# Moving two buffers to the upper end of SBUF and re-planning the Strassen steps of the output projection, in a one-core decoder block

## The chip, the core and the metric

The kernel runs on one core of one Trainium2 chip. The metric is device microseconds of one execution of the whole block. In what follows PE is the matmul engine, DVE the vector engine, ACT the scalar engine, POOL the GpSimd engine (here it mostly issues DMAs), and SP the queue that issues the weight loads. SBUF is the on-chip memory (128 partitions; sizes below are per partition), PSUM the matmul accumulators.

## The reference

One decoder block on 256 tokens of width 4096, all float32:

```python
h = rmsnorm(x, norm_w)
proj = h @ w_in                                  # 4096 -> 20480
u_p, z_p, u_c, b_c, c_c, z_c, g_logit = split(proj)
y_pool = causal_multiscale_pool(u_p, pool_w, pool_scale) * silu(z_p)
y_conv = b_c * causal_conv3(c_c * u_c, conv_w, conv_b) * silu(z_c)
br = [y_pool @ w_branch[0], y_conv @ w_branch[1]]   # 2048 -> 4096 each
merged = sum(sigmoid(g_logit + gate_b) * br)
out = rmsnorm(x + merged @ w_out, final_norm_w)
```

Nearly all of the arithmetic is in the three projections: `w_in`, `w_branch` and `w_out`.

## The kernel before

**Units and steps.** Each projection is cut into units of 1024 output columns; a unit is a run of steps, and a step is one pair of 128-row slices of the contraction against 256 tokens and 1024 columns. There are 20 units of 16 steps for `w_in` (`cz`, `cb`, `cu`, `cc`, `pz`, `pu`, `g`), eight units of 8 steps for `w_branch` (`b0_c`, `b1_c`) and four of 16 steps for `w_out` (`o0` to `o3`). Every float32 operand is split into a rounded high part and a low rest, and a product is three matmuls (high by high, high by low, low by high). A step is of one of two kinds. A "P" step is plain: 8 blocks of 128x128 against 512 columns, so 24 matmuls. An "S" step is a Strassen step (Winograd's form): 7 products, so 21 matmuls, at the price of four sums of weight quarters that DVE makes. The strings at the head of the file (`NINE`, `TEN`, `OUT3`, ...) give the kinds in order; `TEN` has ten S steps of 16, `NINE`, `NINE_A` and `NINE_B` nine, `EIGHT` eight, the old `OUT3` seven.

**Standing operands.** The activations stand in the array (they are the weights in the sense of the engine: LDWEIGHTS loads them, 128x128 at a time), and the weight matrices stream past out of `ring`. The activation operands lie in `arena`, 16 of them at a time: eight with room for a P step (4 KB each), six with 7 KB and two with 8 KB. The very last one has its own tile `last_pair` (8 KB), which is on the right side of SBUF, so it lies at the top end. An S step on one of the P-sized operands finds its four Strassen sums in the tile `side` (4 KB), which holds them for one operand at a time. Of the six with 7 KB, the first unit finds one block each in `extra` (6 KB), a tile that is closed after step 12.

**Places.** The pool `const` holds, in this order, `arena` 82 KB, `ring` 60, `raw` 24, `E` 8, `Y` 8, `sa` 4, `ident` 0.5 and `par` 0.4, together 187 KB. Pools opened later lie behind it: first `extra`, then `parts` (8 KB, the Strassen sums of the weights) and behind that `side`. So counted from the start of the tiles, `arena` and `ring` are the first 142 KB, and `extra`, `parts` and `side` begin at 187 KB or above.

**Weights.** SP loads 1 MB of weights per step into one of three `raw` buffers. ACT rounds it into cells of `ring` (15 cells), DVE writes the low rest beside it. For an S step DVE also makes the sums (`parts<-raw`, `parts<-parts,raw`), ACT rounds them and DVE writes their low rests. The order on ACT and DVE is fixed by the program (`pump` lays down the work up to four steps ahead of the matmul steps, as far as cells and `raw` buffers are free). A `tick` is six matmuls: every six matmuls one item of `queue` is laid down; `queue` holds a unit's epilogue, a list of items and empty places (`gap(n)`), which so runs while the next unit is multiplied.

**Joining a unit with S steps.** The four corner products (`shared` banks) are copied out by ACT into a slot, `corner_sums` combines them there with three DVE instructions, and `combine` adds the slot to the base. There are two ways. With `rotates`, the slot is the next `raw` buffer in its turn, and DVE adds it (`add(d4, d4, q)`). With `late` and not `rotates`, the slot is `Y` or `last_pair`, and two accumulating DMAs on POOL's queue (`gather`, seen as `E<-Y`) do the addition. Before the change all four out units rotate and are added by DVE.

**Side sums.** `side_items(i)` loads the columns of operand `i` (`sa<-in_xc`, POOL's queue), scales them (ACT), forms the four sums (`sums_s`, four DVE instructions) and writes high and low parts to `side` (ACT, DVE). It is run for operand 7 in the epilogue of `cz0`, for use in the `NINE` units; `pz0` then closes `side` for other tiles. In the epilogue of `g0_0`, while `g1_0` is multiplied, it runs for operand 6 and then for operand 7, each followed by a store to `side_d` in DRAM; the `TEN` units then reload one of the two between their first and last S step.

**The out units.** `o0` has SIX5 (six S steps), `o1` and `o2` EIGHT, `o3` OUT3. The epilogue gathers the rows of `x` onto `E` (`row`), takes the sums of squares (`square`, ACT), multiplies by the final norm's weights in `Y[:, 0]` and stores to `o_d`. `start` loads these weights into `Y[:, 0]`, three quarters into the unit. The last three P steps of `o3` are the tail, run first for tokens 0 to 127 and then for the others, each followed by `finish`.

Of the kernel before, what the change touches and what calls it, by code (L numbers as in the profile page):

```python
# [9 lines left out]
F32 = mybir.dt.float32  # L10
# [32 lines left out]
NINE_B = "PSPSPSPSSPSSPSPS"  # L43
HOST = "PPPBPPMMPSPSSPSSPSS"
TEN = "PSPSSPSSPSSPSSPS"
OUT3 = "PSPSPSPSPSPSSPPP"
B0 = "PPPPSPSP"
B1 = "PSPSPSPP"
B1_LAST = "PSPPSPPP"
# [3 lines left out]
def hybrid_block(ctx: ExitStack, tc: tile.TileContext, x, xc, prm, rows_in, w_in, pool_w, w_branch, w_out, out):  # L53
# [17 lines left out]
    def sub(dst, a, b):  # L71
        return tt(dst, a, b, ALU.subtract)
# [10 lines left out]
    def move(dst, src):  # L83
        return pin(nc.gpsimd.dma_start(dst, src))
# [2 lines left out]
        return pin(nc.gpsimd.dma_start(dst, src, accum_op=ALU.add))  # L87

    const = ctx.enter_context(tc.tile_pool(name="const", bufs=1))
    PSUM = bass.MemoryType.PSUM  # L90
    psum = ctx.enter_context(tc.tile_pool(name="psum", bufs=1, space=PSUM))
    dram = ctx.enter_context(tc.tile_pool(name="dram", bufs=1, space=bass.MemoryType.DRAM))

    def sb(name, shape, dt=F32):
        return const.tile(shape, dt, name=name)

    arena = sb("arena", [P, (4 * ND + 7 * NS + 8 * (NB - 1)) * KB], F32R)
    ring = sb("ring", [P, CELLS, 2, NH], F32R)
    raw = sb("raw", [P, NRAW, 2 * NU])
    E = sb("E", [P, 2, NU])  # L100
    Y = sb("Y", [P, 2, NU])
    sa = sb("sa", [P, 8, P])
    ident = sb("ident", [P, P])
    par = sb("par", [P, 112])
# [131 lines left out]
    def quarters(tile_):  # L236
        return tile_.rearrange("p a (b c) -> p (a b) c", c=NH)
# [239 lines left out]
    def gap(n):  # L477
        return [None] * n
# [38 lines left out]
    def in_unit(name, col, epi, text, **kw):  # L517
        units.append(Unit(name, lambda i: w_in[col // NU, i], seq_x(text), x_ops, epi, scaled=True, **kw))
        units[-1].text = text
        return units[-1]  # L520

    def side_items(i=ND - 1):
        def scaled():
            for k in range(2):
                v = sa[:, 6 - 2 * k:8 - 2 * k]
                act(v, v, scale=norm_col(2 * i + k))

        return [lambda: move(sa[:, 4:].rearrange("p o c -> p (o c)"), xc[i])] + gap(7) + [scaled, None, lambda: sums_s(sa)] + gap(3) + [
            lambda: act(side["tile"][:, 0], sa[:, 0:4]), None,
            lambda: sub(side["tile"][:, 1], sa[:, 0:4], side["tile"][:, 0].bitcast(F32))]  # L530

    def silu_y(late):
        def silu(t):
            act(Y[:, t], Y[:, t], AF.Silu, **(dict(scale=rin[:, t:t + 1]) if late else {}))
        return gap(18 if late else 3) + [lambda: silu(0), None, lambda: silu(1)]
# [5 lines left out]
    def conv_units(c, first):  # L541
        base = 2 * HALF + c * NU

        def b_epi(u):
            def copy(j):
                act(chan(Y)[:, 2 * j:2 * j + 2], bankview(j))
            return gap(6) + transposes(E, copy) + [lambda: move(g_d[c], Y)]

        def c_epi(u):
            def copy(j):  # L550
                if j == 3:
                    for i in range(4):
                        act(chan(E)[:, 2 * i:2 * i + 2], bankview(i))

            def taps(j):
                v, y = chan(E)[:, 2 * j:2 * j + 2], chan(Y)
                for i in range(2):
                    b = 2 * j + i
                    kb = 8 * c + b
                    act(y[:, b], v[:, i], AF.Identity, scale=tap_col(2, kb), bias=bias_col(kb))  # L560
                for s in (1, 2):
                    for i in range(2):
                        b = 2 * j + i
                        kb = 8 * c + b
                        stt(y[:, b, s:], v[:, i, 0:T - s], tap_col(2 - s, kb), y[:, b, s:], ALU.mult, ALU.add)

            items = gap(6) + pairs(transposes(E, copy)) + gap(1)
            for j, n in enumerate((1, 7, 8, 8)):
                items += gap(n) + [lambda j=j: taps(j)]
            return items + [lambda: move(E, g_d[c])] + gap(6) + [lambda: mul(E, E, Y), lambda: put(y_d[1, c], chan(E))]  # L570

        u = in_unit(f"cz{c}", base + 3 * HALF, lambda u: silu_y(u.late) + (gap(4) + side_items() if first else []),
                    FIRST if first else SIX4, dst=Y)
        u.rotates, u.late = first, not first
        in_unit(f"cb{c}", base + HALF, b_epi, NINE_B if c else NINE_A).urgent = lambda: mul(E, E, Y)
        u = in_unit(f"cu{c}", base, lambda u: rescale(Y), EIGHT3, dst=Y)
        u.late, u.rotates = True, False
        in_unit(f"cc{c}", base + 2 * HALF, c_epi, NINE_A).urgent = lambda: mul(E, E, Y)
# [101 lines left out]
    def gate_unit(n, c):  # L680
        def epi(u):
            def bias(t):
                gather(E[:, t], gate_b[n, None, c * NU:(c + 1) * NU].to_broadcast([P, NU]))

            pause = gap(12)
            if (n, c) == (1, 3):
                pause = gap(5) + [lambda: move(Y, gates_d[0, 0])] + gap(6)
            items = (rescale(E) if u.late else gap(1)) + [lambda: bias(0), lambda: bias(1)] + pause + [
                lambda: act(E[:, 0], E[:, 0], AF.Sigmoid), None,
                lambda: act(E[:, 1], E[:, 1], AF.Sigmoid), lambda: move(gates_d[n, c], E)]  # L690
            if (n, c) == (0, 0):
                sides = []
                for i in range(ND - 2, ND):
                    sides += side_items(i) + [lambda i=i: move(side_d[i - ND + 2], side["tile"])]
                items += gap(len(sides) - len(items))
                items = [lambda a=a, b=b: (a and a(), b and b()) for a, b in zip(items, sides + gap(len(items)))]
            return items
        text = HOST if (n, c) == (0, 0) else SEVEN3 if (n, c) == (1, 3) else NINE if (n, c) == (1, 0) else TEN
        u = in_unit(f"g{n}_{c}", 6 * HALF + n * D + c * NU, epi, text)
        u.rotates, u.late = False, (n, c) != (1, 3)  # L700

    def spare():
        return last_pair["tile"].rearrange("p (a n) -> p a n", a=2)
# [30 lines left out]
    def out_unit(c):  # L734
        cs = slice(c * NU, (c + 1) * NU)

        def start():
            move(Y[:, 0], final_w[None, cs].to_broadcast([P, NU]))

        def epi(u):  # L740
            def row(t):
                gather(E[:, t], xrows[:, t, cs])

            def square(t):
                act(Y[:, 1], E[:, t], AF.Square, accum_out=ossq[:, t, c:c + 1])
            return gap(1) + [lambda: row(0), lambda: row(1)] + gap(14) + [
                lambda: square(0), lambda: square(1),
                lambda: mul(E, E, Y[:, 0:1].to_broadcast([P, 2, NU])), lambda: move(o_d[c], E)]

        text = (SIX5, EIGHT, EIGHT, OUT3)[c]  # L750
        units.append(Unit(f"o{c}", lambda i: w_out[c, i], seq_x(text), m_ops, epi, before=start))

    def sums_s(st):
        sub(st[:, Q5], st[:, A21], st[:, A22])
        sub(st[:, Q6], st[:, Q5], st[:, A11])
        sub(st[:, Q7], st[:, A11], st[:, A21])
        add(st[:, Q3], st[:, A12], st[:, Q6])
# [335 lines left out]
    for u in units:  # L1093
        if u.name == "b0_0":
            last_pair["stack"].close()
            open_last(F32)
        if not u.rotates:
            u.join.slot = quarters(Y if u.name[0] == "g" else spare() if u.name[0] == "b" else E)
        if u is names["g1_0"]:
            bands_open.close()  # L1100
            open_side()
        if u is last_x:
            side["stack"].close()
            more = ctx.enter_context(tc.tile_pool(name="more", bufs=1))
            stages.append(more.tile([P, 8, P], F32, name="sb"))
            queue_fills()
        if u is last:
            break
        for st in u.steps:
            assert st.prepared, (u.name, st.kind)  # L1110
            run_step(u, st)
            if u.text is TEN and st.kind == "S" and st.op in x_ops[:ND] and st is not u.steps[-1]:
                move(side["tile"], side_d[ND - 1 - x_ops.index(st.op)])
            state["now"] += 1
            if state["now"] == OPENED:
                opening.close()
                sums = ctx.enter_context(tc.tile_pool(name="parts", bufs=1)).tile([P, 4, NH], F32, name="parts")
                open_side()
            pump()
            if u.before and st is u.steps[len(u.steps) * 3 // 4]:  # L1120
                flush()
                u.before()
        flush()
        combine(u)
        queue.extend(u.epi(u))
        pump()
# [102 lines left out]
```

## Time and profile before

| | us |
|---|---|
| median of 3 runs | 2378.26 (2377.94 to 2379.73) |
| the profiled execution, own time | 2378.31 |
| its span in the profile | 2376.6 |
| PE busy | 2358.6 |
| DVE busy | 2178.6 |
| ACT busy | 1519.3 |
| POOL busy | 116.8 |

The span runs from the first to the last instruction; the own time of the execution is 1.7 us longer. The four busy times are of engines that run beside each other. A busy PE in the profile means that a matmul is in its pipeline, not that matmuls follow each other as closely as they can.

### The profile page before, as it was taken

What the parts mean: (1) busy time and instruction counts of PE and PEld (TensorE: products, weight loads), DVE (VectorE), ACT (ScalarE), POOL (GpSimd) and SP (SyncE); (2) the same over time, 40 slices, a digit from 0 to 9 for tenths busy, and PEclk for the clock granted to TensorE, in tenths of its full rate; (3) what the DMA queues carried; (4) which work ended last, traced back from release to release, by engine and by line L of the source; (5) the groups of instructions that cost most, each with busy time, mean ns of one, the idle gap of its engine ahead of it and who ended that gap; (6) DMA issues with size and microseconds to landing.
All of it is one profiled execution on the core that took longest, in us unless ns stands there. A gap on an engine that the chain in (4) does not pass through costs nothing.

```text
span 2376.6 us, 28235 instructions
## 1 busy us (share of the span) xinstructions
PE 2358.6 (99%) x10466; PEld 1945.8 (82%) x10466; DVE 2178.6 (92%) x2378; ACT 1519.3 (64%) x1801; POOL 116.8 (5%) x181
## 2 busy tenths in 40 slices
PE   9999999999999999999999999999999999999998
PEld 7888888888888888888788888888888888888886
DVE  8889989989989969969899999998898799899998
ACT  6666656756656656656676767667665566566664
POOL 0000000000001000000000000001100000000000
PEclk9999999999999999999999999999999999999999
DMA  9656646756657546746877787778766666767767
GB/s 344 230 193 235 223 164 260 238 191 236 224 178 269 211 174 221 240 174 217 259 248 251 264 260 250 248 272 274 267 253 242 248 237 239 257 211 252 259 218 267
DMA packets 91322, 564.20 MB, mean 237 GB/s; under 512 B 10096, under 2 KB 10352, under 8 KB 30256
## 3 DMA queue, kind: packets, MB, share of 16 engines
q1 hardware_dynamic: 69824, 485.39, 56.5%
q0 software_dynamic: 20784, 75.77, 11.9%
q8 instruction: 82, 1.34, 0.2%
q10 hardware_dynamic: 576, 1.24, 0.1%
q14 instruction: 56, 0.46, 0.1%
HBM read 522.51 MB, written 27.26 MB: 231 GB/s over the span
## 4 chain that ended last, share of the span: by engine, by line
PE 94%; DVE 3%; DMA 1%; ACT 1%; issue 0%; POOL 0%; SPq 0%; DVEq 0%; ACTq 0%; POOLq 0%
PE sums L1021 69%; PE shared L1021 23%; DVE ring L63 1%; PE shared L665 1%; PE shared L458 1%; DMA sa<-in_xc_dram 1%; DVE parts L63 1%; DMA raw<-in_w_in_dram 1%; ACT ring L60 0%; DVE E L63 0%; DVE raw L63 0%; ACT E L60 0%; DVE E L75 0%; ACT raw L60 0%; PE shared L641 0%
## 5 line engine op out<-in xcount | busy, mean ns | idle before, releaser
L1021 PE MATMUL sums<-ring,arena 128*128 128x512 f32 x7215 | 1687.1, 390 | 4.2 <-DVE ring L63 1.8
L1021 PEld LDWEIGHTS sums<-ring,arena 128*128 128x128 f32 x7215 | 1352.8, 188 | 288.4 <-DVE ring L63 3.1
L63 DVE TENSOR_TENSOR ring<-raw,ring 128x1024 fp32r<-128x1024 f32 (+3 forms) x879 | 971.9, 1126 | 137.2 <-ACT ring L60 136.1
L60 ACT ACTIVATE ring<-raw 128x1024 fp32r<-128x1024 f32 (+3 forms) x682 | 796.2, 1202 | 251.7 <-PE sums L1021 101.2
L60 ACT ACTIVATE ring<-parts 128x512 fp32r<-128x512 f32 (+1 forms) x638 | 476.5, 761 | 475.1 <-DVE parts L63 413.8
L1021 PE MATMUL shared<-ring,arena 128*128 128x512 f32 x2169 | 523.2, 389 | 0.3 <-DVE ring L63 0.3
L63 DVE TENSOR_TENSOR ring<-parts,ring 128x1024 fp32r<-128x1024 f32 (+1 forms) x442 | 492.0, 1158 | 6.1 <-ACT ring L60 6.1
L1021 PEld LDWEIGHTS shared<-ring,arena 128*128 128x128 f32 x2169 | 407.0, 188 | 85.5 <-DVE ring L63 0.8
L63 DVE TENSOR_TENSOR parts<-parts,raw 128x512 f32<-128x512 f32 x416 | 286.6, 689 | 0.0
L63 DVE TENSOR_TENSOR parts<-raw 128x1024 f32<-128x1024 f32 x208 | 254.0, 1221 | 5.5 <-DMA raw<-in_w_in_dram 5.4
L1021 PE MATMUL sums<-ring,last_pair 128*128 128x512 f32 x336 | 84.6, 396 | 0.8 <-DVE ring L63 0.8
L1021 PEld LDWEIGHTS sums<-ring,last_pair 128*128 128x128 f32 x336 | 63.1, 188 | 16.3 <-DVE ring L63 1.2
L1021 PE MATMUL shared<-ring,last_pair 128*128 128x512 f32 x192 | 47.6, 397 | 0.0
L1021 PEld LDWEIGHTS shared<-ring,last_pair 128*128 128x128 f32 x192 | 36.1, 188 | 8.7
L60 ACT ACTIVATE E<-sums 128x512 f32<-128x512 f32 x72 | 39.7, 595 | 5.5 <-PE sums L1021 3.6
L60 ACT ACTIVATE E<-sums,rin 128x512 f32<-128x512 f32 x28 | 17.7, 689 | 29.3 <-PE sums L1021 29.3
L1021 PE MATMUL shared<-ring,side 128*128 128x512 f32 x135 | 34.0, 396 | 0.0
L63 DVE TENSOR_TENSOR raw<-raw 128x512 f32<-128x512 f32 (+1 forms) x27 | 23.5, 870 | 9.8 <-ACT raw L60 8.9
L1021 PEld LDWEIGHTS shared<-ring,side 128*128 128x128 f32 x135 | 25.4, 188 | 6.0
L60 ACT ACTIVATE last_pair<-shared 128x512 f32<-128x512 f32 x44 | 23.9, 596 | 9.4 <-PE shared L458 8.9
L63 DVE TENSOR_TENSOR E<-E,Y 128x2048 f32<-128x2048 f32 x13 | 29.8, 2290 | 0.1
L63 DVE TENSOR_TENSOR E<-E,last_pair 128x2048 f32<-128x2048 f32 x12 | 27.4, 2286 | 2.2 <-ACT E L60 2.2
(134 smaller groups left out, 717.1 us busy)
## 6 DMA issues: line engine op xcount, KB each, us to landing
raw<-in_w_in_dram SPq DMA_DIRECT2D x318, 1024.0 KB, 4.9
raw<-in_w_branch_dram SPq DMA_DIRECT2D x64, 1024.0 KB, 4.9
raw<-in_w_out_dram SPq DMA_DIRECT2D x64, 1024.0 KB, 5.1
E<-in_rows_dram POOLq DMA_DIRECT2D x16, 512.0 KB, 9.8
gates_d<-E POOLq DMA_DIRECT2D x8, 1024.0 KB, 6.1
E<-Y POOLq DMA_DIRECT2D x14, 512.0 KB, 8.2
Y<-E POOLq DMA_DIRECT2D x10, 512.0 KB, 8.1
y_d<-E POOLq DMA_DIRECT2D x8, 512.0 KB, 6.4
```

The lines of the kernel that those rows point to most:

```text
L60: return pin(nc.scalar.activation(dst, src, func, **kw))
L63: return pin(nc.vector.tensor_tensor(out=dst, in0=a, in1=b, op=op))
L458: pin(nc.tensor.transpose(shared(j)[:, i * T + t * P:i * T + (t + 1) * P], src[:, t, c:c + P], ident))
L665: pin(nc.tensor.matmul(o, a, b, start=(k, i) == (0, 0), stop=(k, i) == (3, 2)))
L1021: pin(nc.tensor.matmul(ps, lhs, rhs, start=n == 0, stop=n == u.total[b] - 1))
```

## The change

It has four parts.

1. `raw` and `Y` (32 KB) leave `const` for a pool on the right side of SBUF, at its upper end. `const` is 155 KB then, so `extra`, `parts` and `side` lie 32 KB lower, and `last_pair`, which is also on the right, lies 32 KB lower too, under the two.
2. `side_items` now always ends with a store to `side_d`. The sums of operand 7 are stored in the epilogue of `cz0`. In the epilogue of `g0_0` only operand 6 is computed, after a gap of 14 ticks, stored, and operand 7 is reloaded.
3. `o0`, `o1`, `o2` no longer rotate: their slot is `Y`, and they are joined by accumulating DMAs. `start` moves into their epilogue (tick 16), and the squares from tick 17 to tick 25.
4. `o1` and `o2` get `NINE` in place of `EIGHT`, and `o3` eight S steps in place of seven, three of them in a row before the tail. For the ninth, `o1` computes the side sums of the merged activations' operand 7 while it is multiplied; `more` (a stage for operands) is closed to make room.

```diff
-OUT3 = "PSPSPSPSPSPSSPPP"
+OUT3 = "PSPSPSPSSPSSSPPP"
...
+    upper = ctx.enter_context(tc.tile_pool(name="upper", bufs=1, side="right"))
...
-    raw = sb("raw", [P, NRAW, 2 * NU])
+    raw = upper.tile([P, NRAW, 2 * NU], F32, name="raw")
     E = sb("E", [P, 2, NU])
-    Y = sb("Y", [P, 2, NU])
+    Y = upper.tile([P, 2, NU], F32, name="Y")
...
+    def side_load(i):
+        move(side["tile"], side_d[i - ND + 2])
+
-    def side_items(i=ND - 1):
+    def side_items(i):
...
-            lambda: sub(side["tile"][:, 1], sa[:, 0:4], side["tile"][:, 0].bitcast(F32))]
+            lambda: sub(side["tile"][:, 1], sa[:, 0:4], side["tile"][:, 0].bitcast(F32)),
+            lambda: move(side_d[i - ND + 2], side["tile"])]
...
             if (n, c) == (0, 0):
-                sides = []
-                for i in range(ND - 2, ND):
-                    sides += side_items(i) + [lambda i=i: move(side_d[i - ND + 2], side["tile"])]
-                items += gap(len(sides) - len(items))
+                sides = gap(HUSH) + side_items(ND - 2) + [lambda: side_load(ND - 1)]
...
-            return gap(1) + [lambda: row(0), lambda: row(1)] + gap(14) + [
+            return gap(2) + [lambda: row(0), lambda: row(1)] + gap(12) + [start] + gap(8) + [
                 lambda: square(0), lambda: square(1),
                 lambda: mul(E, E, Y[:, 0:1].to_broadcast([P, 2, NU])), lambda: move(o_d[c], E)]
 
-        text = (SIX5, EIGHT, EIGHT, OUT3)[c]
-        units.append(Unit(f"o{c}", lambda i: w_out[c, i], seq_x(text), m_ops, epi, before=start))
+        text = (SIX5, NINE, NINE, OUT3)[c]
+        u = Unit(f"o{c}", lambda i: w_out[c, i], seq_x(text), m_ops, epi, before=start if c == 3 else None)
+        u.late, u.rotates = c < 3, c == 3
+        units.append(u)
...
-            u.join.slot = quarters(Y if u.name[0] == "g" else spare() if u.name[0] == "b" else E)
+            u.join.slot = quarters(Y if u.name[0] in "go" else spare() if u.name[0] == "b" else E)
+        if u is names["o1"]:
+            assert not fills
+            more.close()
+            open_side()
+
+            j, items = ND - 1, list(queue)
+            queue.clear()
+            sides = (gap(HUSH) + [lambda: move(sa[:, 4:].rearrange("p o c -> p (o c)"),
+                                                   m_d[j // 4][:, j % 4].rearrange("p k t -> p (k t)"))] + gap(8) + [
+                lambda: sums_s(sa), None, None, lambda: act(side["tile"][:, 0], sa[:, 0:4]), None,
+                lambda: sub(side["tile"][:, 1], sa[:, 0:4], side["tile"][:, 0].bitcast(F32))])
+            items += gap(len(sides) - len(items))
+            sides += gap(len(items) - len(sides))
+            queue.extend([lambda a=a, b=b: (a and a(), b and b()) for a, b in zip(items, sides)])
```

More of the change, by code (lines that the diff above doesn't have):

```diff
@@ L570, in c_epi @@
             return items + [lambda: move(E, g_d[c])] + gap(6) + [lambda: mul(E, E, Y), lambda: put(y_d[1, c], chan(E))]
-        u = in_unit(f"cz{c}", base + 3 * HALF, lambda u: silu_y(u.late) + (gap(4) + side_items() if first else []),
+        u = in_unit(f"cz{c}", base + 3 * HALF, lambda u: silu_y(u.late) + (gap(4) + side_items(ND - 1) if first else []),
                     FIRST if first else SIX4, dst=Y)
@@ L1103, in hybrid_block @@
             side["stack"].close()
-            more = ctx.enter_context(tc.tile_pool(name="more", bufs=1))
-            stages.append(more.tile([P, 8, P], F32, name="sb"))
+            more = ExitStack()
+            ctx.enter_context(more)
+            stages.append(more.enter_context(tc.tile_pool(name="more", bufs=1)).tile([P, 8, P], F32, name="sb"))
             queue_fills()
@@ L1112, in hybrid_block @@
             if u.text is TEN and st.kind == "S" and st.op in x_ops[:ND] and st is not u.steps[-1]:
-                move(side["tile"], side_d[ND - 1 - x_ops.index(st.op)])
+                side_load(2 * ND - 3 - x_ops.index(st.op))
             state["now"] += 1
```

## The prediction

> **What bounds the kernel now.** I read the page's busy times and its chain first, then the matmul groups with shapes kept apart, then PE's timeline inside one undisturbed unit, then the stretches unit by unit, and last the waits where a unit took longer than its count of matmuls.
>
> ```profile
> PE 2358.6 (99%) x10466; PEld 1945.8 (82%) x10466; DVE 2178.6 (92%) x2378; ACT 1519.3 (64%) x1801; POOL 116.8 (5%) x181
> PE 94%; DVE 3%; DMA 1%; ACT 1%; issue 0%; POOL 0%; SPq 0%; DVEq 0%; ACTq 0%; POOLq 0%
> ```
>
> PE is never idle for long and holds 94% of the chain, so only three things can move the time: fewer matmuls, matmuls that follow each other more closely, and the few places where PE waits. DVE at 92% is the engine that can turn into the bound.
>
> The groups of matmuls, by the tile that stands in the array (columns: count, then busy time and mean duration):
>
> ```profile
> L1021 PE MATMUL sums<-ring,arena 128*128 128x512 f32 x7215 | 1687.1, 390 | 4.2 <-DVE ring L63 1.8 <-ACT E L60 1.4 <-DVE ring L760 1.1
> L1021 PE MATMUL shared<-ring,arena 128*128 128x512 f32 x2169 | 523.2, 389 | 0.3 <-DVE ring L63 0.3
> L1021 PE MATMUL sums<-ring,last_pair 128*128 128x512 f32 x336 | 84.6, 396 | 0.8 <-DVE ring L63 0.8
> L1021 PE MATMUL shared<-ring,last_pair 128*128 128x512 f32 x192 | 47.6, 397 | 0.0
> L1021 PE MATMUL shared<-ring,side 128*128 128x512 f32 x135 | 34.0, 396 | 0.0
> L1021 PE MATMUL sums<-ring,side 128*128 128x512 f32 x45 | 13.0, 396 | 0.0
> L1021 PE MATMUL sums<-ring,extra 128*128 128x512 f32 x36 | 10.4, 396 | 0.0
> ```
>
> All are 128x128 against 512 columns from `ring`. With `arena` standing one takes 389 to 390 ns, with `last_pair`, `side` or `extra` 396 to 397. These three tiles have nothing in common but their place: behind 187 KB of tiles or at the top end, where `arena` and `ring` lie in the first 142 KB. Durations overlap in the pipeline, so the cost is read from the starts (columns: start, time, then count). Near the end of unit `g1_2`:
>
> ```profile
> 1429.07 2.88 PE L1021 MATMUL shared<-ring,arena 128*128 128x512 f32 x12
> 1431.79 0.84 PE L1021 MATMUL sums<-ring,arena 128*128 128x512 f32 x3
> 1432.47 1.56 PE L1021 MATMUL sums<-ring,last_pair 128*128 128x512 f32 x6
> 1433.88 2.98 PE L1021 MATMUL shared<-ring,last_pair 128*128 128x512 f32 x12
> 1436.69 0.86 PE L1021 MATMUL sums<-ring,last_pair 128*128 128x512 f32 x3
> 1437.39 6.32 PE L1021 MATMUL sums<-ring,arena 128*128 128x512 f32 x27
> 1443.55 0.86 PE L1021 MATMUL sums<-ring,side 128*128 128x512 f32 x3
> ```
>
> Twelve on `arena` take 1431.79 - 1429.07 = 2.72 us, 226.7 ns each; twelve on `last_pair` 1436.69 - 1433.88 = 2.81 us, 234.2 ns. So 7.5 ns more each. The 27 behind them on `arena` take 6.16 us where 27 x 226.7 ns is 6.12, so a little (0.04 us) spills over onto what follows.
>
> The stretches of single units (columns: length, then PE, PEld, DVE, ACT, POOL busy):
>
> ```profile
> 1121.11:1205.78 84.67, 82.38 (x358) 66.71 (x357) 76.32 (x89) 56.64 (x70) 7.04 (x9) 1.00 0.75 243
> 1205.78:1286.43 80.65, 80.65 (x356) 66.46 (x354) 80.58 (x90) 56.85 (x71) 5.31 (x6) 1.00 0.78 255
> ...
> 2119.26:2201.01 81.75, 81.75 (x361) 67.58 (x360) 77.00 (x82) 51.96 (x64) 2.88 (x4) 1.00 0.70 240
> ...
> 2282.81:2365.10 82.29, 82.29 (x364) 67.94 (x362) 77.37 (x85) 47.80 (x61) 3.58 (x5) 1.00 0.73 258
> ```
>
> These are `g1_0`, `g0_1`, `o1` and `o3`. In `g0_1` DVE is busy 80.58 of 80.65 us and PE still never idles: a full DVE is not yet a stall. `g1_0` has three matmuls more than `g0_1` (357 against 354 weight loads), worth 0.68 us, but takes 4.02 us more: 3.3 us are lost there. Why, the chain and the waits of that unit say:
>
> ```profile
> 1128.08 14.92 DMA sa<-in_xc_dram
> ...
> 1143.08 0.91 ACT L60 ACTIVATE sa<-sa,par 128x256 f32<-128x256 f32 x2 [8.08 <-DMA sa<-in_xc_dram]
> ...
> 1145.40 0.69 DVE L63 TENSOR_TENSOR ring<-raw,ring 128x512 fp32r<-128x512 f32 x1 [7.35 <-ACT ring L60]
> ...
> PE sums L1021 <- DVE ring L63: 1.9, 3, 0.8
> ```
>
> The load of `sa` for the side sums is queued on POOL behind the two joining transfers of `g0_0` and lands 14.9 us after its issue. ACT, which works in order, waits 8.08 us for it with the scaling, DVE then waits 7.35 us for ACT's rounding of weights, and PE runs dry in the steps after.
>
> **Part 1: places.** The slow tiles serve 336 + 192 + 135 + 45 + 36 = 744 matmuls; at 7.5 ns that is 5.6 us, and with a part of what spills over behind 24 runs on `last_pair` (24 x 0.04 = 1.0 at most) I take 6.0. All of it is on the path, since PE is the path. The change moves each of the three tiles down by the 32 KB of `raw` and `Y`. Counted from the start of the tiles `extra` comes to 155 KB and `side` to 163. Before, `const`, `parts`, `side` and `last_pair` stood at once, 187 + 8 + 4 + 8 = 207 KB, so the top is at 207 or little above, and `last_pair` comes to about 168 to 176. The rows show fast places up to 142 KB and slow ones from 187 to the top; the tiles land between, so the bounds are 0 and -6.6 us. There are two levels and no slope (389 or 390 anywhere in 142 KB, 396 or 397 in all three high tiles), which looks like a border and not like distance. Every slow tile is shifted by 32 KB, one and a half times the 20 KB that are seen slow; they all clear the border if the slow stretch at the top is no longer than 32 KB. That it is so short is my choice and not a reading; where it is longer, `last_pair` with 528 of the 744 matmuls is the first to stay in it, and that is the second rival below. The two side steps that `o1` and `o2` gain add no slow matmuls then.
>
> The Trainium skill, "SBUF — State Buffer", section "SBUF size: 192, 224, or 256?", gives 192 KiB of memory per partition for trn1, 224 for trn2, and 16 KiB of that reserved. If the added 32 KiB were the slow part, the border would be at 176 KB of the tiles by these figures (an estimate from that page), `last_pair` would end right under it, and the whole 6.0 would come. The page says nothing of speed, and no tile of the trace that PE multiplies with in its steps lies between 142 and 187 KB.
>
> What goes up is `raw` and `Y`, which PE does not read in its steps. DVE and ACT do; `parts`, which now lies high, is the nearest row for what that costs:
>
> ```profile
> L63 DVE TENSOR_TENSOR ring<-raw,ring 128x1024 fp32r<-128x1024 f32 x515 | 617.2, 1222 | 13.0 <-ACT ring L60 12.7
> L63 DVE TENSOR_TENSOR ring<-parts,ring 128x1024 fp32r<-128x1024 f32 x390 | 460.7, 1221 | 6.1 <-ACT ring L60 6.1
> ```
>
> The same shape takes 1222 ns from the low `raw` and 1221 ns from the high `parts`: I cost the move of the buffers at nothing on DVE.
>
> **Part 2: side sums.** In `g1_0` the second set of sums goes (four small subtractions and one of 128x512 on DVE, 1.7 us there by the rows of part 4), and the scaling comes at tick 22 instead of tick 8. A tick is six matmuls, 1.36 us, so it falls 30 us after the unit's start at 1121.11, in place of 11, while the load still leaves POOL's queue right behind the joining transfers, near 1128, and lands near 1143. ACT's 8.08 us, DVE's 7.35 and so PE's 3.3 us go; DVE had only 76.32 us of work in that unit, so nothing else is late next. Bounds: 0 and -3.4; I take -3.3. Added on POOL: one store in `cb0`, and the reload of `side`, which waits for the store before it and holds up `gates_d<-E` behind it, with some 30 us left to the next writer of `E`; `side` itself is needed only in the last step of `g1_0`. I cost these at nothing.
>
> **Part 3: joins by transfer.** The three DVE additions go (2.28 us each), and the `raw` buffer that the join took is free for weights. PE does not wait at these three boundaries now, so this only makes room on DVE. `E` is complete later, but the squares are later too, by 8 ticks or 11 us.
>
> **Part 4: three more S steps.** Each takes 21 matmuls in place of 24: 9 x 226.7 ns = -2.04 us. DVE pays. What a P and an S step cost it, from consecutive starts in `o2`, and the small pieces:
>
> ```profile
> 2236.26 2.36 DVE L63 TENSOR_TENSOR ring<-raw,ring 128x1024 fp32r<-128x1024 f32 x2
> 2238.53 1.22 DVE L63 TENSOR_TENSOR parts<-raw 128x1024 f32<-128x1024 f32 x1
> ...
> 2244.88 2.35 DVE L63 TENSOR_TENSOR ring<-raw,ring 128x1024 fp32r<-128x1024 f32 x2
> ...
> L63 DVE TENSOR_TENSOR sa<-sa 128x128 f32<-128x128 f32 x60 | 14.7, 287 | 0.8 <-ACT sa L60 0.2
> L63 DVE TENSOR_TENSOR side<-sa,side 128x512 fp32r<-128x512 f32 x3 | 2.1, 687 | 0.0
> L63 DVE TENSOR_TENSOR E<-E,raw 128x2048 f32<-128x2048 f32 x3 | 6.9, 2284 | 0.0
> ```
>
> P: 2238.53 - 2236.26 = 2.27 us. S: 2244.88 - 2238.53 = 6.35 us, against 21 x 226.7 ns = 4.76 us on PE. A P turned into an S costs DVE 4.08 us more. `o1`: 77.00 + 4.08 - 2.28 (join) + 1.7 (side sums: 4 x 0.287, overlapped to 1.0, and 0.69) = 80.5 us, of 357 x 226.7 ns = 80.9 us on PE: full, as in `g0_1`, but not over. `o2` has 1.7 less. `o3`: 77.37 + 4.08 - 2.28 = 79.2 of 81.6, but three S steps in a row stand before the tail. There, before:
>
> ```profile
> 2340.23 2.37 DVE L63 TENSOR_TENSOR ring<-parts,ring 128x1024 fp32r<-128x1024 f32 x2
> ...
> 2345.40 2.88 PE L1021 MATMUL shared<-ring,arena 128*128 128x512 f32 x12
> ...
> 2357.25 0.69 DVE L63 TENSOR_TENSOR E<-sums,E 128x512 f32<-128x512 f32 x1 [1.54 <-PE sums L1021]
> ...
> 2365.51 0.69 DVE L63 TENSOR_TENSOR E<-sums,E 128x512 f32<-128x512 f32 x1 [0.64 <-PE sums L1021]
> ```
>
> DVE finishes the last S step's sums at 2342.60; PE needs the first of them from the fourth product, 0.68 us into the twelve at 2345.40: 3.5 us of room. After the change DVE comes there 4.08 - 2.28 = 1.8 us later and PE 0.68 us earlier: 1.0 us of room stays, no stall. In the tail DVE was 1.54 us early at the first half; it is then 1.8 late against PE's 0.68 early, so the first half is finished 0.26 us later than before, and the last one, which had 0.64 us to wait for PE, gains about 0.4 instead of 0.68: +0.3. For `o1`, whose side sums again stand on DVE before a transfer that is queued behind four accumulating ones, I add 0.4 of a possible 0 to 3.4 (the loss in `g1_0`): its sums come 31 us after the unit's start, the transfer should land there by 25 to 37.
>
> **Sum**, against the profiled execution's own 2378.31 us (its span plus 1.7; the median of the runs shown is 2378.26, the same): -6.0 - 3.3 - 2.04 + 0.3 + 0.4 = -10.6, so 2367.7 us. The unknown ends give 2366 to 2370 for this case.
>
> **Rivals.**
>
> *A wait of the old kind comes back* (in `o1` before the side sums, or in `o3` at the three S steps, or the loss in `g1_0` stays). For it: the transfer in `o1` is behind more traffic than the one in `g1_0`, and DVE has 0.4 us to spare in that unit. Against: 14 ticks of gap, and room on DVE from the join. Price about the same loss as in `g1_0`: 2367.7 + 3.3 = 2371.0.
>
> *The tiles do not land in the fast part*, so the change does not do what it says. For it: no row between 142 and 187 KB. Against: the shift is longer than the stretch seen slow. 2367.7 + 6.0 = 2373.7. The Trainium skill, "TensorE: Matmul & The Clock Gate", section "Step-by-step: what each phase is for", gives the standing operand its own SBUF read port and lets its load run under the matmul before; by that rule the place would not matter at all and this would be the time. The trace disagrees: 234.2 against 226.7 ns.
>
> *Slower: DVE reads `raw` more slowly in its new place.* DVE is full in the five `TEN` units; what it reads from `raw` in them is
>
> ```profile
> L63 DVE TENSOR_TENSOR ring<-raw,ring 128x1024 fp32r<-128x1024 f32 (+2 forms) x169 | 169.1, 1021 | 2.5 <-ACT ring L60 2.5
> L63 DVE TENSOR_TENSOR parts<-parts,raw 128x512 f32<-128x512 f32 x100 | 68.9, 689 | 0.0
> L63 DVE TENSOR_TENSOR parts<-raw 128x1024 f32<-128x1024 f32 x49 | 59.9, 1222 | 0.0
> ```
>
> 298 us (1205.78 to 1609). Each per cent more would go straight onto the path there, 3.0 us, so the gain is used up from 3.6% on; at 5% the time is 2367.7 + 14.9 = 2382.6. Against it stands the pair 1222 and 1221 ns above.
>
> **How the numbers follow.** Forecast 0.63, a new or remaining wait 0.17, tiles still slow 0.13, slower 0.05, a larger gain 0.02. A measurement of this kernel can tell about 0.2%, 4.8 us, from no change, so faster means under 2373.5: the forecast, the first rival, the larger gain and a small part of the second, 0.85; within 0.2% is the rest of the second with an edge of the third, 0.10; slower 0.05. The range runs from the low end of the forecast to the second rival, 2366.0 to 2373.7.
>
> **What would show it.** Right: one mean duration, 389 to 390 ns, for all matmuls of 512 columns whatever stands; `g1_0` at about 81 us with no ACT wait on `sa<-in_xc`; `o1` and `o2` near 81 us with DVE full; 204 matmuls on `side` (24 more), 10457 in all. Wrong: 396 ns on `last_pair` or `side`; DVE means above 1222 ns from `raw`; PE waits on `ring` in `o1` or in the last S steps of `o3`.

## The result and the profile after

| | before | after |
|---|---|---|
| median, us | 2378.57 (2377.71 to 2381.04, 22 runs) | 2374.04 (2372.96 to 2377.54, 22 runs) |
| ratio, 95% interval | | 0.9983 (0.9977 to 0.9989) |
| profiled execution, own time | 2378.31 | 2374.06 |
| span | 2376.6 | 2372.2 |

The change is faster by 4.5 us between the medians; the ratio puts it at 0.17%. The forecast was 2367.7 us, 10.6 us less than before, so 6 us of it did not come. The busy times and the groups of matmuls by standing tile, after:

```profile
PE 2355.7 (99%) x10457; PEld 1944.9 (82%) x10457; DVE 2185.2 (92%) x2389; ACT 1525.0 (64%) x1804; POOL 124.4 (5%) x188
...
L1025 PE MATMUL sums<-ring,arena 128*128 128x512 f32 x7179 | 1679.1, 390 | 3.0 <-ACT E L60 1.4 <-DVE ring L764 1.0 <-DVE ring L63 0.6
L1025 PE MATMUL shared<-ring,arena 128*128 128x512 f32 x2175 | 524.6, 389 | 0.0
L1025 PE MATMUL sums<-ring,last_pair 128*128 128x512 f32 x321 | 81.0, 396 | 0.0
L1025 PE MATMUL shared<-ring,last_pair 128*128 128x512 f32 x204 | 50.6, 397 | 0.0
L1025 PE MATMUL shared<-ring,side 128*128 128x512 f32 x153 | 38.5, 396 | 0.0
L1025 PE MATMUL sums<-ring,side 128*128 128x512 f32 x51 | 14.7, 396 | 0.0
```

There are nine matmuls fewer, as counted. But the tiles that moved 32 KB down are as slow as before: 396 to 397 ns on `last_pair` and `side`. The largest term of the prediction's sum did not come at all. The stretch of `o2` before (the others before are in the prediction), and then those of `g1_0`, `o1`, `o2` and `o3` after (length, then PE, PEld, DVE, ACT, POOL busy):

```profile
2201.01:2282.81 81.80, 81.80 (x362) 67.58 (x361) 76.62 (x80) 51.79 (x63) 2.87 (x4) 1.00 0.69 238
```

```profile
1121.00:1202.21 81.21, 81.21 (x359) 67.05 (x357) 78.56 (x89) 58.15 (x70) 6.38 (x8) 1.00 0.81 264
...
2115.83:2197.04 81.21, 81.21 (x358) 67.04 (x357) 80.07 (x90) 53.84 (x66) 5.86 (x7) 1.00 0.77 258
2197.04:2278.26 81.22, 81.22 (x358) 67.03 (x357) 78.62 (x85) 53.43 (x66) 5.31 (x6) 1.00 0.75 253
2278.26:2359.83 81.57, 81.57 (x361) 67.35 (x359) 77.96 (x87) 48.45 (x60) 6.56 (x8) 1.00 0.77 260
```

`g1_0` gained 84.67 - 81.21 = 3.46 us, `o1` 0.54, `o2` 0.58, `o3` 0.72, and PE is busy through all four. That is 5.3 us; the span gained 4.4, so 0.9 us were given back at the end, in the tail. There DVE adds the joined corner sums (`E<-E,parts`) and then finishes the halves of the last tiles. After:

```profile
2351.21 2.29 DVE L63 TENSOR_TENSOR E<-E,parts 128x2048 f32<-128x2048 f32 x1
...
2353.60 0.69 DVE L63 TENSOR_TENSOR E<-sums,E 128x512 f32<-128x512 f32 x1
...
2361.14 0.68 DVE L63 TENSOR_TENSOR E<-sums,E 128x512 f32<-128x512 f32 x1
...
2343.71 16.51 PE L1025 MATMUL sums<-ring,arena 128*128 128x512 f32 x72
```

The last matmuls before:

```profile
2363.91 1.57 PE L1021 MATMUL sums<-ring,last_pair 128*128 128x512 f32 x6
```

Before, both of these additions (`E<-sums,E`) waited for PE (1.54 and 0.64 us); now neither waits: DVE is the late one. The last matmul ends at 2360.22 us and the span 12.0 us later; before, it ended at 2365.48 us, 11.1 us before the end of the span.

### The profile page after: what moved, and what is told of

Same layout as the page of the kernel before. It is cut to its first block, busy times and chain, and to the rows that moved or that the text cites. A ratio compares the mean times of both kernels' runs of the same rounds, so it can differ in the third digit from the quotient of the medians.

```text
span 2372.2 us, 28256 instructions
## 1 busy us (share of the span) xinstructions
PE 2355.7 (99%) x10457; PEld 1944.9 (82%) x10457; DVE 2185.2 (92%) x2389; ACT 1525.0 (64%) x1804; POOL 124.4 (5%) x188
## 4 chain that ended last, share of the span: by engine, by line
PE 95%; DVE 3%; ACT 1%; DMA 1%; issue 0%; SPq 0%; DVEq 0%; ACTq 0%
PE sums L1025 69%; PE shared L1025 23%; DVE ring L63 1%; PE shared L670 1%; PE shared L459 1%; DVE parts L63 1%; DVE E L63 1%; DMA raw<-in_w_in_dram 1%; ACT ring L60 0%; DVE raw L63 0%; DVE E L75 0%; DMA raw<-in_w_out_dram 0%; ACT E L60 0%; ACT raw L60 0%; PE shared L646 0%
## 5 line engine op out<-in xcount | busy, mean ns | idle before, releaser
L60 ACT ACTIVATE ring<-parts 128x512 fp32r<-128x512 f32 (+1 forms) x647 | 483.4, 761 | 471.6 <-DVE parts L63 410.4
L63 DVE TENSOR_TENSOR ring<-parts,ring 128x1024 fp32r<-128x1024 f32 (+1 forms) x449 | 500.1, 1161 | 6.2 <-ACT ring L60 6.1
L63 DVE TENSOR_TENSOR parts<-parts,raw 128x512 f32<-128x512 f32 x422 | 292.6, 693 | 0.0
L63 DVE TENSOR_TENSOR parts<-raw 128x1024 f32<-128x1024 f32 x211 | 258.6, 1225 | 9.2 <-DMA raw<-in_w_in_dram 5.2
L87 POOL DMA_DIRECT2D E<-Y x20 | 24.3, 1454 | 366.5 <-DVE Y L63 322.6
L60 ACT ACTIVATE Y<-shared 128x512 f32<-128x512 f32 x56 | 30.4, 602 | 4.1 <-PE shared L459 3.4
L63 DVE TENSOR_TENSOR Y<-Y 128x512 f32<-128x512 f32 (+1 forms) x33 | 28.7, 869 | 1.7 <-ACT Y L60 0.2
```

The lines of the kernel that those rows point to most:

```text
L60: return pin(nc.scalar.activation(dst, src, func, **kw))
L63: return pin(nc.vector.tensor_tensor(out=dst, in0=a, in1=b, op=op))
```

## The experiments

**First question: what makes a standing tile slow?** The prediction had read it as place. But the compiled kernels' addresses show a second thing that the slow tiles have in common. `arena` (16512) and `ring` (100480) both start on a multiple of 128 bytes, 128 past a multiple of 256. `extra` and `side` start 192, and `last_pair` 224 bytes past a multiple of 256, before the change and after it, because 32 KB is a multiple of 256. Three kernels with a few bytes of padding tried that, and one tried the side sums alone.

*Kernel before, starts on multiples of 128:*

```diff
     ossq = sb("ossq", [P, 2, 5])
+    sb("pad", [P, 16])
...
+    upper = ctx.enter_context(tc.tile_pool(name="upper", bufs=1, side="right"))
+    upper.tile([P, 24], F32, name="top")
```

> The kernel before with two empty paddings: 64 bytes at the end of the pool const and 96 bytes at the upper end of SBUF. The high tiles stay high (extra, parts and side move up by 64 bytes, last_pair down by 96), but their start addresses become multiples of 128 bytes, as those of arena and ring are. Before, extra and side began 64 bytes and last_pair 96 bytes past such a multiple. Theory A (alignment: a standing operand that does not start on a multiple of 128 bytes is slow, wherever it lies): all 128x512 matmuls at 389 to 390 ns, none at 396, and 744 x 7.5 ns plus the spill-over, 5.6 to 6.6 us, gone: about 2372.3 us. Theory B (place: a border somewhere between 142 and 155 KB of tiles): 396 ns stays on extra, side and last_pair, time as before, 2378.5 us. Theory C (the tiles are slow because they are tiles of their own, apart from arena): as theory B.

Measured: 2374.95 us (11 runs), ratio 0.9987 (0.9978 to 0.9996) to the kernel before, which took 2378.21 us beside it.

```profile
L1024 PE MATMUL sums<-ring,last_pair 128*128 128x512 f32 x336 | 82.3, 389 | 0.8 <-DVE ring L63 0.8
L1024 PE MATMUL shared<-ring,last_pair 128*128 128x512 f32 x192 | 46.1, 389 | 0.0
L1024 PE MATMUL shared<-ring,side 128*128 128x512 f32 x135 | 34.0, 396 | 0.0
L1024 PE MATMUL sums<-ring,side 128*128 128x512 f32 x45 | 13.1, 399 | 0.0
L1024 PE MATMUL sums<-ring,extra 128*128 128x512 f32 x36 | 10.4, 396 | 0.0
```

`last_pair` is fast at the very top of SBUF: theories B and C fall, and the two paddings gain 3.3 us, not the 6 us of theory A. But `side` and `extra` stay slow on a multiple of 128, so theory A falls too. `last_pair` now lay 128 past a multiple of 256, as `arena` and `ring` do; `side` and `extra` lay on a multiple of 256.

*Changed kernel, the same paddings:*

> The changed kernel with the same two paddings (64 bytes at the end of const, 96 bytes at the upper end), so that extra, side and last_pair start on multiples of 128 bytes in their new places. Theory A (alignment): all at 389 to 390 ns; 765 matmuls on these tiles now (321 + 204 + 153 + 51 + 36), so 5.7 to 6.7 us less than the changed kernel: about 2367.8 us. Theory B (place) and theory C (own tile): 396 ns stays and the time is that of the changed kernel, 2374.0 us.

Measured: 2370.91 us (6 runs), ratio 0.9970 (0.9958 to 0.9981). Again `last_pair` at 389 and `side` at 396 to 399 ns: 3.1 us less than the changed kernel, half of theory A's figure.

*Changed kernel, `arena` 64 bytes off:*

```diff
+    sb("pad0", [P, 16])
     arena = sb("arena", [P, (4 * ND + 7 * NS + 8 * (NB - 1)) * KB], F32R)
+    sb("pad1", [P, 16])
     ring = sb("ring", [P, CELLS, 2, NH], F32R)
```

> The changed kernel with arena moved up by 64 bytes, so that it starts 64 bytes past a multiple of 128; a second padding of 64 bytes behind it keeps ring on a multiple of 128. Nothing else moves by other than 128 bytes. Theory A (alignment): the 9354 matmuls on arena slow down from 389-390 to 396 ns, 7.5 ns each, and the time rises by about 70 us, to about 2444 us. Theories B (place) and C (own tile): no change, 2374.0 us.

Measured: 2394.63 us (4 runs), ratio 1.0069 (1.0055 to 1.0083).

```profile
L1027 PE MATMUL sums<-ring,arena 128*128 128x512 f32 x7179 | 1694.6, 392 | 4.0 <-DVE ring L63 1.8 <-ACT E L60 1.3 <-DVE ring L766 0.8
L1027 PE MATMUL shared<-ring,arena 128*128 128x512 f32 x2175 | 530.3, 392 | 0.0
```

With the two paddings `arena` moves by 64 bytes and `ring` by 128, so `arena` now starts 192 bytes past `ring`, modulo 256. The matmuls on `arena` get slower, 392 against 389 to 390 ns, and the kernel by 20.6 us (2.2 ns for each of 9354), not by 70. So the start address acts on `arena` too, by an amount that depends on where it is.

*Kernel before, side sums alone* (the edit is part 2 of the change):

> The kernel before with part 2 of the change alone: the side sums of operand 7 are stored once and reloaded, and in the epilogue of g0_0 only operand 6 is computed, after 14 ticks. By the account of the prediction ACT's wait of 8.1 us for the load of sa goes, g1_0 takes 81.2 us instead of 84.7, and the whole gains 3.3 to 3.5 us: 2375.0 us. If the loss in g1_0 had another cause (DVE overfull there), less than half of that is gained.

Measured: 2374.90 us (11 runs), ratio 0.9988 (0.9980 to 0.9997), 3.3 us under the kernel before. `g1_0` in it:

```profile
1120.79:1202.00 81.21, 81.21 (x358) 67.02 (x357) 78.57 (x89) 58.16 (x70) 6.38 (x8) 1.00 0.80 263
```

84.67 became 81.21 us, and ACT's scaling of `sa` no longer waits. The account of the stall holds in size and place.

**Second question: the standing operand's own address, or its distance to the moving one?**

*Changed kernel, all standing tiles as `arena` and `ring` modulo 256:*

```diff
     ossq = sb("ossq", [P, 2, 5])
+    sb("pad", [P, 48])
...
     upper = ctx.enter_context(tc.tile_pool(name="upper", bufs=1, side="right"))
+    upper.tile([P, 24], F32, name="top")
```

> The changed kernel with paddings of 192 bytes at the end of const and 96 at the upper end, so that extra, side and last_pair all start 128 bytes past a multiple of 256, as arena and ring do. In the run before with multiples of 128 only last_pair, which met this, got fast; extra and side, on multiples of 256, stayed at 396 ns. Theory D (phase: the standing operand is fast where its address agrees with the fast tiles' modulo 256): all 128x512 matmuls at 389 to 390 ns, about 2 us less than the run aligned to 128, near 2369 us, 5.7 to 6.7 us under the changed kernel's profile. Theory A (multiples of 128) and theory E (last_pair got fast for another reason, side and extra are slow by themselves): side and extra stay at 396 ns, time as in the run aligned to 128, 2370.9 us.

Measured: 2367.73 us (2367.30 to 2368.91, 5 runs), ratio 0.9955 (0.9941 to 0.9968).

```profile
L1027 PE MATMUL shared<-ring,last_pair 128*128 128x512 f32 x204 | 49.0, 389 | 0.0
L1027 PE MATMUL shared<-ring,side 128*128 128x512 f32 x153 | 37.4, 389 | 0.0
L1027 PE MATMUL sums<-ring,extra 128*128 128x512 f32 x36 | 10.1, 389 | 0.0
...
1420.47 2.88 PE L1027 MATMUL shared<-ring,arena 128*128 128x512 f32 x12
1423.19 0.84 PE L1027 MATMUL sums<-ring,arena 128*128 128x512 f32 x3
...
1425.23 2.88 PE L1027 MATMUL shared<-ring,last_pair 128*128 128x512 f32 x12
1427.95 0.84 PE L1027 MATMUL sums<-ring,last_pair 128*128 128x512 f32 x3
```

One duration for all, and the starts agree: twelve matmuls in 2.72 us on `arena` and 2.72 us on `last_pair`, where `last_pair` took 2.81 us before. The whole term of the prediction (6.0 us) comes: 6.3 us less than the changed kernel's median. Theories A and E fall. Below, "in phase" stands for this: all standing tiles start where `arena` and `ring` do, modulo 256.

*Changed kernel, `arena` and `ring` both 64 bytes off* (the padding ahead of `arena` alone):

> The changed kernel with 64 bytes of padding ahead of arena and none behind it, so arena and ring both move by 64 bytes: to 192 past a multiple of 256, and still equal to each other. Theory D1 (what counts is the difference between the standing operand's address and ring's, modulo 256): matmuls on arena stay at 389 to 390 ns, time as the changed kernel's, 2374 us. Theory D2 (what counts is the standing operand's own address modulo 256): arena is slow as in the run where it alone moved by 64 bytes, about 2.5 ns per matmul, 20 us more: 2394 us.

Measured: 2373.08 us (10 runs), ratio 0.9978 (0.9969 to 0.9987).

```profile
L1026 PE MATMUL sums<-ring,arena 128*128 128x512 f32 x7179 | 1679.0, 390 | 2.7 <-ACT E L60 2.0 <-DVE ring L765 0.7
L1026 PE MATMUL shared<-ring,arena 128*128 128x512 f32 x2175 | 524.6, 389 | 0.0
```

`arena` stays at 389 to 390 ns. Theory D2, which gave 2394, falls.

*Changed kernel, `ring` 128 bytes off:*

```diff
+    sb("pad1", [P, 32])
     ring = sb("ring", [P, CELLS, 2, NH], F32R)
```

> The changed kernel with 128 bytes of padding between arena and ring: arena stays where it is, ring moves by 128 bytes, to a multiple of 256. Theory D1 (difference to ring): every matmul on arena slows down as those on side did at a difference of 128, by 7.5 ns, 9354 of them, about 70 us: 2444 us. Theory D2 (own address): nothing changes on arena, 2374 us.

Measured: 2421.79 us (4 runs), ratio 1.0181 (1.0167 to 1.0195).

```profile
L1026 PE MATMUL sums<-ring,arena 128*128 128x512 f32 x7179 | 1717.5, 395 | 1.4 <-DVE ring L765 1.0 <-ACT E L60 0.4
L1026 PE MATMUL shared<-ring,arena 128*128 128x512 f32 x2175 | 537.2, 395 | 0.0
L671 PE MATMUL shared<-ring 128*128 128x512 f32 x96 | 22.1, 389 | 0.0
```

`arena` has not moved, `ring` and what lies behind it have moved by 128 bytes, and the kernel loses 47.8 us against the changed one: 5.1 ns per matmul on `arena`. The direction is theory D1's, the size was guessed too high (70 us). One rival is left: in both kernels with a slow `arena`, `ring` itself starts on a multiple of 256, so the moving operand's own address could be the cause. The last line answers it: in these 96 matmuls both operands lie in `ring`, at distance 0, and they take 389 ns as in every other kernel. With the run before it, this shows that the distance between the standing and the moving operand counts, modulo 256. It does not give the whole size: at a distance of 128, `arena` takes 395 ns here, while `side` and `extra` took 396 to 399 in the first of these kernels.

**Third question: the tail.** *All in phase, and the eight S steps of `o3` spread:*

```diff
-OUT3 = "PSPSPSPSSPSSSPPP"
+OUT3 = "PSPSSPSPSSPSSPPP"
```

> The kernel with all standing tiles in phase (192 and 96 bytes of padding), and besides the eight S steps of o3 in the order PSPSSPSPSSPSSPPP instead of PSPSPSPSSPSSSPPP, so that two and not three stand in a row before the tail. In the changed kernel's profile DVE enters the tail late and finishes the last half 1.3 us after the last matmul began, against 0.4 before. If the three S steps in a row cause that, DVE comes 1.6 us earlier, and the time is 0.5 to 0.9 us under that of the same kernel with the old order; if DVE is late for its total work in o3, there is no difference.

Measured: 2367.89 us (2366.14 to 2369.09, 5 runs), ratio 0.9953 (0.9941 to 0.9966). The 0.5 to 0.9 us expected do not show in the medians (2367.73 with three in a row); the profiles do separate the two tails. The last half of the last tile, in the kernel in phase with three S steps in a row and then in the spread one:

```profile
2354.46 0.68 DVE L63 TENSOR_TENSOR E<-sums,E 128x512 f32<-128x512 f32 x1
```

```profile
2355.38 0.69 DVE L63 TENSOR_TENSOR E<-sums,E 128x512 f32<-128x512 f32 x1 [0.19 <-PE sums L1027]
```

In the spread order DVE waits for PE again (0.19 us). From the end of the last matmul to the end of the span it is 11.2 us against 12.1. So the third S step in a row, not DVE's total work, is what costs the tail about 1 us; that the whole kernel gains it is not shown by the times.

**Fourth question: what part 1 does.** *Kernel before, in phase, nothing else* (paddings of 192 and 96 bytes):

> The kernel before with nothing but paddings of 192 bytes at the end of const and 96 at the upper end: extra, side and last_pair stay at the top of SBUF (203 KB and above, the reserved 16 KB counted) but agree with ring modulo 256. Theory D1 (difference to ring modulo 256): 389 to 390 ns for all, 6.0 us less, the size that the prediction gave to part 1: 2372.4 us. Theory B (place): 396 ns on extra and side, time at least that of the kernel before with multiples of 128, 2375 us.

Measured: 2372.49 us (11 runs), ratio 0.9975 (0.9966 to 0.9984), 389 ns on `side`, `extra` and `last_pair`:

```profile
L1024 PE MATMUL sums<-ring,last_pair 128*128 128x512 f32 x336 | 82.3, 389 | 0.8 <-DVE ring L63 0.8
L1024 PE MATMUL shared<-ring,side 128*128 128x512 f32 x135 | 33.1, 389 | 0.0
L1024 PE MATMUL sums<-ring,extra 128*128 128x512 f32 x36 | 10.1, 389 | 0.0
```

The tiles are all at the top of SBUF there. So 288 bytes of padding on the kernel before gain 5.8 us, more than the whole change did.

*Changed kernel, `raw` and `Y` back in `const`:*

> The changed kernel with part 1 undone: raw and Y are back in const, everything else is as changed, with no padding. Theory D1: side, extra and last_pair lie 64 and 96 bytes off ring's phase with part 1 and without it, so part 1 does nothing: 2374.0 us, the changed kernel's time. Theory B, or a cost of raw and Y at the upper end: a difference of 1 us or more in either direction.

Measured: 2373.95 us (11 runs), ratio 0.9983 (0.9974 to 0.9991): the changed kernel's own ratio, and the slow tiles are as slow as with part 1:

```profile
L1024 PE MATMUL shared<-ring,last_pair 128*128 128x512 f32 x204 | 50.6, 397 | 0.0
L1024 PE MATMUL shared<-ring,side 128*128 128x512 f32 x153 | 38.5, 396 | 0.0
```

Part 1 does nothing by itself that these runs can tell.

Back to the third question. *Changed kernel, all in phase, old order of `o3`:*

> The changed kernel in phase (192 and 96 bytes of padding) with the old order of o3, seven S steps and two in a row before the tail. It has three matmuls more than the changed kernel in phase (0.68 us). If the third S step in a row costs the tail about 1 us, as the spread order showed, the old order is 0.2 to 0.4 us better: 2367.4 us, with 11.5 us from the last matmul's start to the end in place of 12.6. If the tail is late for the joins or the later squares, it is 0.7 us worse.

Measured: 2367.54 us (2366.74 to 2369.15, 5 runs), ratio 0.9956 (0.9943 to 0.9968). In its profile the last addition again waits 0.55 us for PE, and the span ends 11.1 us after the last matmul, against 12.1 with three in a row. The difference of 0.2 us to the new order is within the scatter: the eighth S step of `o3` neither gains nor loses what these runs can tell. The three changed kernels in phase, at 2367.5 to 2367.9 us, beat both the kernel before and the changed one.

## Why the prediction was wrong

*Part 1, places: -6.0 forecast, 0 measured. This is the step that failed.* The size was right, as the kernels in phase show (6.3 us on the changed kernel, 5.8 on the kernel before), and so was the reading of the slow tiles from their starts. The cause was wrong. The prediction said that `extra`, `side` and `last_pair` "have nothing in common but their place". They had: each starts at another phase than `ring`, 64 or 96 bytes off modulo 256, and a shift by 32 KB keeps that. Place was ruled out by `last_pair`, fast at the top of SBUF, and the change's part 1 by the run that undid it. The prediction had also argued that two levels without a slope look like a border; they look the same for a phase, and the sizes in the code that would have told (`par` with 448 bytes, the small tiles behind it) were in front of the reader. The Trainium skill, "TensorE: Matmul & The Clock Gate", section "Step-by-step: what each phase is for", has two independent read ports, so that loading the next weights takes no read bandwidth from the running matmul. The run that moved `ring` does not fit that: 395 ns against 389 to 390 on an unmoved `arena`, 47.8 us in all.

*Part 2, side sums: -3.3 forecast, -3.46 in the profile, -3.3 alone.* Right in mechanism, place and size. The load of `sa` still took 15.8 us to land in `g1_0`; the scaling came later and did not wait.

*Part 3, joins: nothing forecast, nothing found at the three boundaries.* PE is busy through `o1`, `o2` and `o3`.

*Part 4, three S steps: -2.04 forecast, -1.84 in the units (0.54 + 0.58 + 0.72).* The rest is the new side steps of `o1` and `o2`, 24 matmuls at the slow spacing. DVE was full in `o1` (80.07 of 81.21 us; 80.5 forecast) without a stall, so the 0.4 us added for a wait there did not come.

*The tail: +0.3 forecast, +0.9 measured.* The mechanism, DVE late for the first half, was the forecast one; the size was not. DVE finished adding the corner sums 75.2 us after the start of `o3` (2353.50 - 2278.26), where it had been ready after 72.9 before (2357.25 - 1.54 - 2282.81): 2.3 us later, not the 1.8 of the sum. In the kernel with the S steps of `o3` spread, which has as many of them, the span ends 11.2 us after the last matmul, about as before, so it is the order and not the added work alone that sets this delay.

*The rival "DVE reads `raw` more slowly in its new place":* its sign came, but not its cause. In the changed kernel's profile the mean for `raw` is 1226 ns, above the 1222 before; for `parts` it is 1225, above 1221:

```profile
L63 DVE TENSOR_TENSOR ring<-raw,ring 128x1024 fp32r<-128x1024 f32 x513 | 616.6, 1226 | 12.3 <-ACT ring L60 11.8
L63 DVE TENSOR_TENSOR ring<-parts,ring 128x1024 fp32r<-128x1024 f32 x395 | 467.5, 1225 | 5.6 <-ACT ring L60 5.5
```

In the changed kernel in phase, `raw` lies in the same new place and the mean is 1219 ns:

```profile
L63 DVE TENSOR_TENSOR ring<-raw,ring 128x1024 fp32r<-128x1024 f32 x513 | 614.0, 1219 | 12.2 <-ACT ring L60 11.7
```

So the place does not explain the rise; what does is open. It cost nothing that the stretches show: `g0_1`, one of the units in which the rival put the loss, takes 80.65 us after as before.

The rival "the tiles do not land in the fast part" gave 2373.7 us and came within 0.4 us. That is luck: it too took place for the cause, and the tiles did not stay slow for where they lie.

## What to carry to other kernels

When one group of matmuls is some nanoseconds slower than its like, list the exact start addresses of both operands modulo 256 before explaining it by place: here a few bytes of padding decided 6 us, and 128 bytes in the wrong spot cost 48. For matmuls like these (128x128 standing against 512 float32 columns, with a new standing operand each time; no run tried another form) put the tiles that PE loads as weights and the tiles that it streams at the same offset modulo 256, and put odd-sized small tiles behind them. A late engine that had waited in the tail before the change has exactly that wait as its reserve: sum it to the end of the program, not only to the last matmul.

## What the runs showed of the hardware that was not expected

In these kernels the time of a 128x512 float32 matmul depends on the distance of the standing tile's start from the moving one's, modulo 256 bytes. Mean durations by that distance (standing start minus moving start, from the compiled addresses), from the rows of the profiles:

| distance | tile, kernel | mean, ns |
|---|---|---|
| 0 | `arena` before and after; all tiles of the kernels in phase | 389 to 390 |
| 0 | `last_pair` with starts on multiples of 128 | 389 |
| 32 | `last_pair`, `arena` and `ring` 64 off | 395 to 396 |
| 64 | `side`, `extra`, before and after | 396 |
| 64 | `side`, `extra` with `arena` 64 off and with `ring` 128 off | 392 to 395 |
| 96 | `last_pair`, before and after | 396 to 397 |
| 128 | `side`, `extra` with starts on multiples of 128 | 396 to 399 |
| 128 | `arena` with `ring` 128 off | 395 |
| 192 | `arena` 64 off | 392 |
| 224 | `last_pair`, `arena` 64 off | 395 |

Distance 0 was fast in every case and every other distance was slow, but the same distance (64, 128) did not always give the same mean, so something else has a part in the size. Why the distance counts at all is open (a conflict of the two reads in the memory would fit); no run tried it.

A second thing concerns the clock. In `b1_0`, which the change does not touch, PE waits 1.35 us for a copy of ACT's before, and 1.41 us after. In the profiled execution of the kernel in phase with the spread order the wait is 1.89 us, and the granted clock (the last column but two) is low behind it:

```profile
1723.00:1726.00 3.00, 1.29 (x6) 0.75 (x4) 3.00 (x5) 1.73 (x4) 0.20 (x1) 1.00 0.78 251
1726.00:1729.70 3.70, 3.52 (x9) 2.77 (x10) 3.63 (x5) 3.48 (x6) 0.33 (x1) 0.55 0.87 328
```

In the kernel in phase with three S steps in a row the wait was as long, and the clock stayed at 1.00. The 30 matmuls behind the wait, there and then in the spread order:

```profile
1725.84 7.10 PE L1027 MATMUL sums<-ring,arena 128*128 128x512 f32 x30 [1.94 <-ACT E L60]
```

```profile
1726.18 8.70 PE L1027 MATMUL sums<-ring,arena 128*128 128x512 f32 x30 [1.89 <-ACT E L60]
```

So the low clock cost 1.6 us. In the profile of the kernel before with the side sums alone the same 30 matmuls take 8.74 us behind a wait of 2.13 us (granted clock 0.89 over the 15 us around them), and that execution is 2.2 us above the median of its kernel. The scatter among executions goes with the clock in the changed kernel too: of its 22 runs the five longest (2375.55 to 2377.54 us) are the five with a mean granted clock of 0.997, and the others have 0.998 or 0.999. What decides whether the clock falls behind the wait is open; no run here took the wait away.
